# Seven-product pairs, halved plain pairs and residual rows kept in memory in the gate/up blocks of a hybrid decoder layer

## The chip, the cores and the metric

The kernel runs on one core of one Trainium2 chip. The metric is the device time of one execution in microseconds (us). The engines are TensorE (PE, and PEld for its weight loads), VectorE (DVE), ScalarE (ACT), GpSimd (POOL) and SyncE (SP, which here only issues transfers). Each engine runs its own instructions in a fixed order and waits on semaphores for the others.

## The reference

One decoder layer on 256 tokens of width 2048, in float32. The change touches the last two thirds of it:

```python
y = jnp.concatenate([y_lru, y_ret], axis=-1)
h = h + jnp.einsum('bse,ed->bsd', y, w_out[l])
u = rmsnorm(h, ln2_w[l])
ff = jax.nn.silu(jnp.einsum('bsd,df->bsf', u, w_ffn_gate[l])) * jnp.einsum('bsd,df->bsf', u, w_ffn_up[l])
h = h + jnp.einsum('bsf,fd->bsd', ff, w_ffn_down[l])
return rmsnorm(h, final_norm_w)
```

`w_out` is 2048 x 2048, gate and up are 2048 x 5632 each, `w_ffn_down` is 5632 x 2048. Ahead of it come a norm, one projection to 6144 columns, a gated linear recurrence and a chunked retention.

## The kernel before

**A product is three matmuls.** To keep float32 precision, every operand is split into a high part (a cast on ScalarE to a reduced format, `wh` for weights) and a low part (a subtraction on VectorE, `wl`), line 112 and line 113. A product of two tiles is then three matmuls, high x high, high x low and low x high (`three`, lines 670 to 672), each 128x128 of activations against 128x512 of weights.

**Blocks.** The output projection has blocks 0 and 1, gate/up has blocks 2 to 12 (11 blocks of 512 gate and 512 up columns), and the down projection has two more. A block goes through eight pairs of 256 weight rows. Such a pair is a 2x2 product: activations a11, a12, a21, a22 (two token tiles, two row tiles) against weights b11, b12 (gate), b21, b22 (up). A pair's weights come from memory as two loads of 128x1024 (512 KB each) into `raw` tiles, six buffers in a ring. The split makes `wh` and `wl` tiles of 128x1024; there are four buffers of each (pool `split`), and a buffer is free when the last matmul that reads it is done.

**Plain and seven-product pairs.** A plain pair ("p") is eight products, 24 matmuls. A pair in `SUMMED` is done with seven products, 21 matmuls, in two steps:
- "s" (class `Shared`, method `share`): four products, 12 matmuls, whose sums over all seven-product pairs of a block are needed in several outputs. They are done one block ahead of their own block. Both halves of the weights are loaded; b11 is split, VectorE then makes four sums of halves in place (`add`, line 648), and t1 with t3 (one 128x1024 tile), t2 (in the other half of b11's tile) and t4 (a tile of its own, `t4h`, `t4l`) are split.
- "d" (class `Direct`, method `direct`): three products, 9 matmuls, in the block itself. The second half of the weights is loaded and split once more (one 128x1024 tile); t4 is still there.

`STEPS` has one string for each block, which says in which order its own plain and direct steps and the next block's shared steps stand. The blocks 3 to 10 alternate `"pspsdpsdpsdp"` and `"psdpsdpsddp"`, with three and four seven-product pairs. A block ends with `post`: four operations on VectorE and two on ScalarE on the shared sums (lines 782 to 787), and the gate (lines 842 and 844).

**Order.** Steps are put into `program` in order, loads run three ahead of the step that needs them, and a scheduler then orders each engine's instructions. SyncE issues the weight loads in order; each waits until its raw buffer was read by its last subtraction.

**Residual rows.** `htok`, eight 128x512 float32 tiles (pool `resid`, 16 KB of each partition), hold the residual stream. They are last read in the first plain step of block 2 (transposed by `turn`) and not again before the down projection adds into them (line 888). At block 2 (`swap`) the pools of the recurrence are closed, and a pool `late` is opened for the norm weights `fw`, which SyncE loads.

Of the kernel before, what the change touches and what calls it, by code (L numbers as in the profile page):

```python
# [14 lines left out]
P = 128  # L15
# [13 lines left out]

SUMMED = ((), (4, 5), (2, 3)) + ((1, 2, 3), (0, 1, 2, 3)) * 4 + ((1, 2, 3), (1, 2, 3))
SUMMED_OUT, SUMMED_FFN = (4, 5), (0, 1, 2, 3)

PLAIN = ((4, 5, 6, 7, 0, 1, 2, 3),) * 2 + (tuple(range(8)),) * 11
STEPS = ("pppspppspp", "ppspdpsdpp", "pdpsdpspspp") + ("pspsdpsdpsdp", "psdpsdpsddp") * 4 + ("psdpsdpsdpp", "psdpsdpsdpp")


EARLY_DOWN = (0, 1, 2)
# [5 lines left out]
def tile_hymba_layer(ctx: ExitStack, tc: tile.TileContext, A: dict, out: bass.AP):  # L45
# [2 lines left out]

    cpool = ctx.enter_context(tc.tile_pool(name="consts", bufs=1))
    apool = ctx.enter_context(tc.tile_pool(name="acts", bufs=60))  # L50
    xpool = ctx.enter_context(tc.tile_pool(name="resid", bufs=8))
    rpool = ctx.enter_context(tc.tile_pool(name="raw", bufs=6))
    wpool = ctx.enter_context(tc.tile_pool(name="split", bufs=4))
    early = ctx.enter_context(ExitStack())
    epool = early.enter_context(tc.tile_pool(name="conv", bufs=2))
    tpool = early.enter_context(tc.tile_pool(name="tmp", bufs=6))
    late = []
    pmm = ctx.enter_context(tc.tile_pool(name="pmm", bufs=4, space=PSUM))
    paux = ctx.enter_context(tc.tile_pool(name="paux", bufs=4, space=PSUM))

# [7 lines left out]
        return apool.tile([P, 512], dt, tag="act", name=nm(name))  # L68

    def res_tile(name, dt=F32):  # L70
        return xpool.tile([P, 512], dt, tag="xh", name=nm(name))

    def late_tile(name, dt=F32):
        return late[0].tile([P, 512], dt, tag="late", name=nm(name))
# [40 lines left out]
    class Unit:  # L115
# [6 lines left out]
            self.h, self.l = [], []  # L122

        def load(self, j):
            raw = rpool.tile([P, 1024], F32, tag="raw", name=nm("raw"))
            h = wpool.tile([P, 1024], F32R, tag="wh", name=nm("wh"))
            l = wpool.tile([P, 1024], F32R, tag="wl", name=nm("wl"))
            n = 1024 // self.pieces
            for p in range(self.pieces):
                o = p * n  # L130
                nc.sync.dma_start(out=raw[:, o : o + n], in_=self.src[:, j * 1024 + o : j * 1024 + o + n])
                if self.before:
                    self.before(j * self.pieces + p)
            for p in range(self.pieces):
                o = p * n
                split(h[:, o : o + n], l[:, o : o + n], raw[:, o : o + n])
                if self.after:
                    self.after(j * self.pieces + p)
            self.h.append(h)
            self.l.append(l)  # L140
# [424 lines left out]
    v2 = cpool.tile([P, 2], F32, name="v2")  # L565
    turns = []

    def out_post(d):
# [12 lines left out]

        def post(c, ps):
            cb, t = 2 * d + int(c[2]) - 1, int(c[1]) - 1
            h = htok[cb, t]
            v.tensor_tensor(out=h, in0=ps, in1=h, op=ALU.add)
            act.activation(out=act_tile("junk"), in_=h, func=AF.Square, accum_out=sq2[:, t, cb : cb + 1])
            if t:
                turns.extend(lambda p=p: turn(p) for p in (2 * cb, 2 * cb + 1))
            if (cb, t) == (3, 1):
                v.tensor_reduce(out=v2, in_=sq2, axis=mybir.AxisListType.X, op=ALU.add)  # L590
                rsqrt_small(r2_tok, v2, 1.0 / D, 2)

        return post
# [10 lines left out]
    class Quad:  # L604
# [19 lines left out]
                self.parts[name] = h[:, n * 512 : n * 512 + 512], l[:, n * 512 : n * 512 + 512]  # L624

        def load(self, half):
            r = rpool.tile([P, 1024], F32, tag="raw", name=nm("raw"))
# [12 lines left out]
            self.add(r)  # L640
            self.cut(("t1", "t3"), self.ra)
            self.cut(("t2", "t4"), r)
# [80 lines left out]
    class Shared(Quad):  # L723
# [2 lines left out]
        hl = None, None  # L726

        def load(self, half):
            r = rpool.tile([P, 1024], F32, tag="raw", name=nm("raw"))
# [17 lines left out]
    class Direct(Quad):  # L747
# [6 lines left out]
            self.shared = shared  # L754

        def load(self, half):
            r = rpool.tile([P, 1024], F32, tag="raw", name=nm("raw"))
            nc.sync.dma_start(out=r, in_=self.src[:, 1024:2048])
            self.cut(("b22", "b21"), r)
            self.parts["t4"] = self.shared.parts["t4"]  # L760

    class Block:

# [26 lines left out]
            for c, a, b in DIRECT:  # L790
                three(self.ps[c], self.lefts[self.summed[m]][a], quad.parts[b], False, False, True)

        def plain(self, i, quad, first, last):
            ps, onto, seen = self.ps, bool(self.summed), set()
            for n, (c, a, b) in enumerate(LAST if last else EIGHT):
                if first and n == 4:
                    while turns:
                        turns.pop(0)()
# [275 lines left out]
    ]  # L1074
    down = Block(NB + 2, lambda i: A["w_down"][i], dl, None, "", EARLY_DOWN, make_left)
    for b, after in zip(blocks, blocks[1:] + [down]):
        if b.index == 2:
            program.append(([], swap))
        b.put(after)
        if b.index == NB:  # L1080
            program.append(([], load_fw))

    for d in range(2):
        down_block(d, down)
# [117 lines left out]
```

## Time and profile before

| | |
|---|---|
| three runs | 1085.74, 1085.87 and 1086.69 us, median 1085.87 |
| span of the profiled execution | 1084.4 us from its first to its last instruction |
| busy TensorE, VectorE, ScalarE | 99%, 88%, 61% of the span |
| granted TensorE clock | 1.00 in every window of 20 us |
| read from memory | 235.26 MB, 219 GB/s over the span |

The profiled execution's own time is its span and what lies around it; against the runs' median that is 1085.87 - 1084.4 = 1.5 us. In the views a line number is that of the kernel; a group is named out<-in by the program's tile names; "idle before" is the engine's own waiting, with what ended it. The timelines give start, length, engine, line, operation and count, and join equal neighbours. TensorE's matmuls overlap, so their lengths add up to more than their time: their price is the distance of their starts. The same holds, by less, for VectorE and ScalarE.

### The profile page before, as it was taken

Reading aid. Unit: us, or ns where it says so; the run is one execution under the profiler, and the core shown is the slowest. Engines: PE = TensorE matmul, PEld = TensorE weight load, DVE = VectorE, ACT = ScalarE, POOL = GpSimd, SP = SyncE. Lnnn points to the kernel's source line nnn. Section 1 sums busy time; section 2 is a strip of 40 time slices with the busy share of each in tenths; the row PEclk is TensorE's granted clock in tenths of the full one; section 3 lists DMA queues with packets and bytes.
Section 4 is the critical chain, followed back from the end, with each engine's and each line's share of the span. In section 5 each row is a group of like instructions: output and inputs, shape, how many; then the busy total and the mean of one; then the engine's idle time right before and its main releaser. Section 6 shows DMA issues by size and latency. Waiting matters only on the chain.

```text
span 1084.4 us, 14584 instructions
## 1 busy us (share of the span) xinstructions
PE 1074.2 (99%) x5101; PEld 899.5 (83%) x5101; DVE 953.5 (88%) x1371; ACT 660.9 (61%) x935; POOL 51.0 (5%) x61
## 2 busy tenths in 40 slices
PE   9999999999999999999999999999999999999997
PEld 7888888888888788888888888888888888888885
DVE  7789799988878889888998998999899899898986
ACT  7666644468746676565566566556556666655563
POOL 0612230000000000000000000000000000000001
PEclk9999999999999999999999999999999999999999
DMA  9964474444565567577677677686675756465652
GB/s 330 333 211 168 160 252 173 174 175 171 181 230 205 184 228 275 198 248 266 220 245 261 220 264 235 233 289 214 233 271 194 265 181 213 171 214 199 212 209 85
DMA packets 69274, 238.32 MB, mean 220 GB/s; under 512 B 7888, under 2 KB 8272, under 8 KB 69200
## 3 DMA queue, kind: packets, MB, share of 16 engines
q1 hardware_dynamic: 68400, 235.29, 62.7%
q0 software_dynamic: 512, 1.57, 0.4%
q8 instruction: 40, 0.66, 0.2%
q10 hardware_dynamic: 288, 0.52, 0.1%
q14 instruction: 34, 0.28, 0.1%
HBM read 235.26 MB, written 2.10 MB: 219 GB/s over the span
## 4 chain that ended last, share of the span: by engine, by line
PE 97%; DVE 1%; issue 1%; DMA 0%; ACT 0%; POOL 0%; SPq 0%; POOLq 0%; ACTq 0%
PE c L670 22%; PE c L672 22%; PE c L671 22%; PE fm L184 11%; PE fm L186 5%; PE tm L164 3%; PE tm L165 3%; PE tm L166 3%; PE p L672 1%; PE p L671 1%; PE p L670 1%; PE ft L833 1%; DMA raw<-in_w_v 0%; PE ht L576 0%; PE sc L482 0%
## 5 line engine op out<-in xcount | busy, mean ns | idle before, releaser
L112 ACT CAST wh<-raw 128x1024 fp32r<-128x1024 f32 (+1 forms) x490 | 460.9, 965 | 362.6 <-PE c L672 132.5
L113 DVE TENSOR_TENSOR wl<-raw,wh 128x1024 fp32r<-128x1024 f32 (+1 forms) x490 | 538.2, 1122 | 91.2 <-ACT wh L112 88.4
L671 PE MATMUL c<-wl,ah 128*128 128x512 f32 x850 | 331.0, 390 | 0.0
L672 PE MATMUL c<-wh,al 128*128 128x512 f32 x850 | 330.4, 389 | 0.0
L670 PE MATMUL c<-wh,ah 128*128 128x512 f32 x850 | 275.0, 391 | 0.2 <-ACT wh L112 0.2
L670 PEld LDWEIGHTS c<-wh,ah 128*128 128x128 f32 x850 | 159.4, 188 | 33.4 <-ACT wh L112 1.1
L672 PEld LDWEIGHTS c<-wh,al 128*128 128x128 f32 x850 | 159.6, 188 | 33.0
L671 PEld LDWEIGHTS c<-wl,ah 128*128 128x128 f32 x850 | 159.6, 188 | 32.7
L184 PE MATMUL fm<-u,wh 128*128 128x512 f32 x512 | 161.3, 396 | 0.0
L186 PEld LDWEIGHTS fm<-u,wl 128*128 128x128 f32 x512 | 96.0, 188 | 22.5
L186 PE MATMUL fm<-u,wl 128*128 128x256 f32 x512 | 101.1, 278 | 0.0
L184 PEld LDWEIGHTS fm<-u,wh 128*128 128x128 f32 x512 | 78.4, 189 | 0.3
L648 DVE TENSOR_TENSOR raw<-raw,raw 128x512 f32<-128x512 f32 x106 | 73.1, 690 | 2.8
L648 DVE TENSOR_TENSOR raw<-raw 128x512 f32<-128x512 f32 x106 | 72.7, 689 | 2.4
L671 PE MATMUL c<-wl,sh 128*128 128x512 f32 x176 | 68.5, 389 | 0.0
L672 PE MATMUL c<-wh,sl 128*128 128x512 f32 x176 | 68.0, 389 | 0.0
L670 PE MATMUL c<-wh,sh 128*128 128x512 f32 x176 | 60.4, 394 | 0.3 <-ACT sh L112 0.3
L165 PE MATMUL tm<-wl,u 128*128 128x512 f32 x128 | 48.8, 394 | 0.0
L166 PE MATMUL tm<-wh,u 128*128 128x512 f32 x128 | 48.7, 390 | 0.0
L164 PE MATMUL tm<-wh,u 128*128 128x512 f32 x128 | 47.3, 398 | 0.8 <-ACT u L288 0.8
L954 POOL TENSOR_TENSOR htok<-htok,fw 128x512 f32<-128x512 f32 x2 | 2.5, 1273 | 895.9 <-ACT junk L947 895.9
L670 PEld LDWEIGHTS c<-wh,sh 128*128 128x128 f32 x176 | 33.1, 188 | 7.3 <-ACT sh L112 0.7
(245 smaller groups left out, 1034.9 us busy)
## 6 DMA issues: line engine op xcount, KB each, us to landing
raw<-in_w_gu SPq DMA_DIRECT2D x212, 512.0 KB, 5.5
raw<-in_w_down SPq DMA_DIRECT2D x91, 512.0 KB, 4.3
raw<-in_w_out SPq DMA_DIRECT2D x34, 512.0 KB, 3.7
raw<-in_w_lx SPq DMA_DIRECT2D x16, 512.0 KB, 6.3
raw<-in_w_k SPq DMA_DIRECT2D x16, 512.0 KB, 3.5
raw<-in_w_q SPq DMA_DIRECT2D x16, 512.0 KB, 4.0
raw<-in_w_rg SPq DMA_DIRECT2D x16, 512.0 KB, 3.4
raw<-in_w_lg SPq DMA_DIRECT2D x16, 512.0 KB, 3.4
```

What stands on the lines that cost most here:

```text
L112: act.copy(out=dst_h, in_=src)
L113: v.tensor_tensor(out=dst_l, in0=src, in1=dst_h.bitcast(F32), op=ALU.subtract)
L164: pe.matmul(ps, ah, wh, start=first, stop=False)
L165: pe.matmul(ps, ah, wl, start=False, stop=False)
L166: pe.matmul(ps, al, wh, start=False, stop=last)
L184: pe.matmul(ps, wh, hl, start=n + i == 0, stop=False)
L186: pe.matmul(ps[:, :S], wl, hl[:, :S], start=False, stop=n + i == len(order) - 1)
L648: v.tensor_tensor(out=dst, in0=a, in1=b, op=ALU.add)
L670: pe.matmul(p, ah, bh, start=first, stop=False, skip_group_check=onto)
L671: pe.matmul(p, ah, bl, start=False, stop=False, skip_group_check=onto)
L672: pe.matmul(p, al, bh, start=False, stop=last, skip_group_check=onto)
L833: pe.transpose(pt[:, o : o + P], g[:, (2 * b + c) * P : (2 * b + c) * P + P], ident)
```

## The change

- `SUMMED`: block 3 has three seven-product pairs, blocks 4 to 11 have four each, block 12 three. Before, blocks 3 to 12 had three and four in turn, and three in 11 and 12.
- `STEPS`: seven blocks, 4 to 10, have the order `"psdhsdhsdhsdhp"`. The new step "h" (class `HalfOf`) is half a plain pair: one load, one split tile, four products, 12 matmuls. Two "h" make one pair.
- Raw tiles: from block 3 to block 11 a second pool `raw2` with six more buffers is used in turn with the first (`raw_tile`).
- Residual rows: in `out_post` each finished tile is also written to memory, `kept_rows`, from ScalarE's queue. The pool `resid` is closed with the others, now at block 3, and makes the room for `raw2`. After block 12 (`swap_back`) `raw2` is closed, and GpSimd's queue loads the eight tiles back and the norm weights after them.
- The split buffers stay four and four; the loads stay three ahead.

The diff, cut:

```diff
-SUMMED = ((), (4, 5), (2, 3)) + ((1, 2, 3), (0, 1, 2, 3)) * 4 + ((1, 2, 3), (1, 2, 3))
+SUMMED = ((), (4, 5), (2, 3), (1, 2, 3)) + ((0, 1, 2, 3),) * 8 + ((1, 2, 3),)
...
-STEPS = ("pppspppspp", "ppspdpsdpp", "pdpsdpspspp") + ("pspsdpsdpsdp", "psdpsdpsddp") * 4 + ("psdpsdpsdpp", "psdpsdpsdpp")
+STEPS = ("pppspppspp", "ppspdpsdpp", "pdpsdpspspp", "pspsdpsdpsdp") + ("psdhsdhsdhsdhp",) * 7 + ("psdpsdpsddp", "psdpsdpsdpp")
...
-    xpool = ctx.enter_context(tc.tile_pool(name="resid", bufs=8))
...
+    xpool = early.enter_context(tc.tile_pool(name="resid", bufs=8))
...
+    def raw_tile():
+        turn_of[0] += 1
+        pool_ = more[0] if more and turn_of[0] % 2 else rpool
+        return pool_.tile([P, 1024], F32, tag="raw", name=nm("raw"))
...
             act.activation(out=act_tile("junk"), in_=h, func=AF.Square, accum_out=sq2[:, t, cb : cb + 1])
+            act.dma_start(out=kept[cb, t], in_=h)
...
+    class HalfOf:
+        n_loads = 1
+
+        def __init__(self, quad, half):
+            self.quad, self.half = quad, half
+
+        def load(self, j):
+            self.quad.load(self.half)
...
-        def plain(self, i, quad, first, last):
+        def plain(self, i, quad, first, last, some=slice(None)):
...
-            for n, (c, a, b) in enumerate(LAST if last else EIGHT):
+            for n, (c, a, b) in enumerate((LAST if last else EIGHT)[some]):
...
+                elif kind == "h":
+                    at = self.steps[:k].count("h") % 2
+                    if not at:
+                        i = plain.pop(0)
+                        whole = Quad(self.src(i), False)
+                    quad = HalfOf(whole, at)
+                    some = slice(4 * at, 4 * at + 4)
+                    run = lambda i=i, quad=whole, some=some: self.plain(i, quad, False, False, some)
...
-            nc.sync.dma_start(out=fw[c], in_=A["final_norm_w"][c * 512 : c * 512 + 512].partition_broadcast(P))
+            pool.dma_start(out=fw[c], in_=A["final_norm_w"][c * 512 : c * 512 + 512].partition_broadcast(P))
...
         early.close()
+        more.append(extra.enter_context(tc.tile_pool(name="raw2", bufs=6)))
...
+    def swap_back():
+        extra.close()
         late.append(ctx.enter_context(tc.tile_pool(name="late", bufs=4)))
+        resid[0] = ctx.enter_context(tc.tile_pool(name="resid2", bufs=8))
+        for key in [(cb, t) for cb in range(4) for t in range(2)]:
+            htok[key] = res_tile("htok")
+            pool.dma_start(out=htok[key], in_=kept[key])
+        load_fw()
```

How the instructions move is shown at two places. The first is VectorE in the middle of a gate/up block of the kernel before: line 113 is a subtraction of a split (`wl_1131` holds t1 and t3, `wl_1136` a direct tile, `wl_1139`, `wl_1142` and `wl_1148` plain tiles), line 648 an add of a shared pair.

```order
L113 TENSOR_TENSOR wl_1128_5452<-raw_1126_5449,wh_1127_5451 128x512
L648 TENSOR_TENSOR raw_1126_5449<-raw_1126_5449 128x512
L648 TENSOR_TENSOR raw_1126_5449<-raw_1126_5449,raw_1129_5464 128x512
L648 TENSOR_TENSOR raw_1129_5464<-raw_1126_5449,raw_1129_5464 128x512
L648 TENSOR_TENSOR raw_1129_5464<-raw_1129_5464 128x512
L113 TENSOR_TENSOR wl_1131_5473<-raw_1126_5449,wh_1130_5472 128x1024
L113 TENSOR_TENSOR wl_1136_5483<-raw_1134_5480,wh_1135_5482 128x1024
L113 TENSOR_TENSOR wl_1128_5452<-raw_1129_5464,wh_1127_5451 128x512
L113 TENSOR_TENSOR t4l_1133_5477<-raw_1129_5464,t4h_1132_5476 128x512
L113 TENSOR_TENSOR wl_1139_5513<-raw_1137_5510,wh_1138_5512 128x1024
L113 TENSOR_TENSOR wl_1142_5519<-raw_1140_5516,wh_1141_5518 128x1024
L113 TENSOR_TENSOR wl_1148_5546<-raw_1146_5543,wh_1147_5545 128x1024
```

VectorE in the same place of the changed kernel, from the second "s" of a block to the third (line 119 is the subtraction now, line 657 the add; `wl_1510` holds t1 and t3, `wl_1515` is the direct tile, `wl_1518` the half plain one):

```order
L119 TENSOR_TENSOR wl_1503_7183<-raw_1501_7180,wh_1502_7182 128x512
L657 TENSOR_TENSOR raw_1501_7180<-raw_1501_7180 128x512
L657 TENSOR_TENSOR raw_1501_7180<-raw_1501_7180,raw_1508_7202 128x512
L657 TENSOR_TENSOR raw_1508_7202<-raw_1501_7180,raw_1508_7202 128x512
L657 TENSOR_TENSOR raw_1508_7202<-raw_1508_7202 128x512
L119 TENSOR_TENSOR wl_1510_7211<-raw_1501_7180,wh_1509_7210 128x1024
L119 TENSOR_TENSOR wl_1515_7230<-raw_1513_7227,wh_1514_7229 128x1024
L119 TENSOR_TENSOR wl_1518_7248<-raw_1516_7245,wh_1517_7247 128x1024
L119 TENSOR_TENSOR wl_1503_7183<-raw_1508_7202,wh_1502_7182 128x512
L119 TENSOR_TENSOR t4l_1512_7215<-raw_1508_7202,t4h_1511_7214 128x512
L119 TENSOR_TENSOR wl_1521_7254<-raw_1519_7251,wh_1520_7253 128x512
```

Between two shared pairs stood two plain tiles, and now stands one: the last row is already the next pair's b11.

The second place is TensorE at the same pair. Before, after the rows of the shared pair (`wh_1130`) and the direct tile (`wh_1135`), come those of a whole plain pair, whose first tile is `wh_1138`:

```order
L670 MATMUL c22_1092_5282<-wh_1130_5472,sh_758_3724 128x512 [waits Activation_49]
L670 MATMUL c21_1093_5286<-wh_1130_5472,sh_758_3724 128x512
L670 MATMUL c11_1018_4939<-wh_1135_5482,ah_755_3715 128x512 [waits Activation_49]
L670 MATMUL c12_1021_4951<-wh_1135_5482,sh_758_3724 128x512
L670 MATMUL c12_1094_5290<-wh_1127_5451,sh_758_3724 128x512 [waits Activation_49]
L671 MATMUL c22_1092_5282<-wl_1131_5473,sh_758_3724 128x512 [waits DVE_49]
L672 MATMUL c22_1092_5282<-wh_1130_5472,sl_759_3725 128x512
```

TensorE in the changed kernel, at the second "s" of a block, where the first row reads b11's cast, `wh_1509` is t1 and t3, `wh_1514` the direct tile and `wh_1517` the half plain one:

```order
L679 MATMUL c11_1504_7186<-wh_1502_7182,ah_741_3677 128x512 [waits Activation_49]
L680 MATMUL c11_1504_7186<-wl_1503_7183,ah_741_3677 128x512 [waits DVE_49]
L681 MATMUL c11_1504_7186<-wh_1502_7182,al_742_3678 128x512
L679 MATMUL c22_1505_7190<-wh_1509_7210,sh_744_3686 128x512 [waits Activation_49]
L679 MATMUL c21_1506_7194<-wh_1509_7210,sh_744_3686 128x512
L679 MATMUL c11_1423_6813<-wh_1514_7229,ah_741_3677 128x512 [waits Activation_49]
L679 MATMUL c12_1426_6825<-wh_1514_7229,sh_744_3686 128x512
L680 MATMUL c22_1505_7190<-wl_1510_7211,sh_744_3686 128x512 [waits DVE_49]
L681 MATMUL c22_1505_7190<-wh_1509_7210,sl_745_3687 128x512
L680 MATMUL c21_1506_7194<-wl_1510_7211,sh_744_3686 128x512
L681 MATMUL c21_1506_7194<-wh_1509_7210,sl_745_3687 128x512
L679 MATMUL c22_1424_6817<-wh_1517_7247,ah_837_4105 128x512 [waits Activation_49]
```

From the last matmul that reads the direct tile of the first "sdh" (`wh_1492`, whose buffer the cast of `wh_1502` takes) to the first that reads the next direct tile (`wh_1514`) are 25 matmuls; from one "s" to the next are 33, where before they were 45.

More of the change, by code (lines that the diff above doesn't have):

```diff
@@ L54, in tile_hymba_layer @@
     early = ctx.enter_context(ExitStack())
+    xpool = early.enter_context(tc.tile_pool(name="resid", bufs=8))
     epool = early.enter_context(tc.tile_pool(name="conv", bufs=2))
     tpool = early.enter_context(tc.tile_pool(name="tmp", bufs=6))
-    late = []
+    late, resid, more, turn_of = [], [xpool], [], [0]
+    extra = ExitStack()
     pmm = ctx.enter_context(tc.tile_pool(name="pmm", bufs=4, space=PSUM))
@@ L70, in res_tile @@
     def res_tile(name, dt=F32):
-        return xpool.tile([P, 512], dt, tag="xh", name=nm(name))
+        return resid[0].tile([P, 512], dt, tag="xh", name=nm(name))
+    def raw_tile():
+        turn_of[0] += 1
+        pool_ = more[0] if more and turn_of[0] % 2 else rpool
+        return pool_.tile([P, 1024], F32, tag="raw", name=nm("raw"))
     def late_tile(name, dt=F32):
@@ L124, in load @@
         def load(self, j):
-            raw = rpool.tile([P, 1024], F32, tag="raw", name=nm("raw"))
+            raw = raw_tile()
             h = wpool.tile([P, 1024], F32R, tag="wh", name=nm("wh"))
@@ L566, in tile_hymba_layer @@
     turns = []
+    kept = nc.dram_tensor("kept_rows", (4, 2, P, 512), F32, kind="Internal").ap()
     def out_post(d):
@@ L626, in load @@
         def load(self, half):
-            r = rpool.tile([P, 1024], F32, tag="raw", name=nm("raw"))
+            r = raw_tile()
             nc.sync.dma_start(out=r, in_=self.src[:, half * 1024 : half * 1024 + 1024])
@@ L728, in load @@
         def load(self, half):
-            r = rpool.tile([P, 1024], F32, tag="raw", name=nm("raw"))
+            r = raw_tile()
             nc.sync.dma_start(out=r, in_=self.src[:, half * 1024 : half * 1024 + 1024])
@@ L756, in load @@
         def load(self, half):
-            r = rpool.tile([P, 1024], F32, tag="raw", name=nm("raw"))
+            r = raw_tile()
             nc.sync.dma_start(out=r, in_=self.src[:, 1024:2048])
@@ L1067, in swap, with stop_more @@
         early.close()
-        late.append(ctx.enter_context(tc.tile_pool(name="late", bufs=4)))
+        more.append(extra.enter_context(tc.tile_pool(name="raw2", bufs=6)))
+    def stop_more():
+        more.clear()
+    def swap_back():
+        extra.close()
+        late.append(ctx.enter_context(tc.tile_pool(name="late", bufs=4)))
+        resid[0] = ctx.enter_context(tc.tile_pool(name="resid2", bufs=8))
[3 more added lines that the diff above has]
+        load_fw()
     blocks = [Block(d, lambda i, d=d: A["w_out"][8 * d + i], y, out_post(d), STEPS[d], SUMMED[d]) for d in range(2)]
@@ L1076, in tile_hymba_layer @@
     for b, after in zip(blocks, blocks[1:] + [down]):
-        if b.index == 2:
+        if b.index == 3:
             program.append(([], swap))
+        if b.index == NB + 1:
+            program.append(([], stop_more))
         b.put(after)
-        if b.index == NB:
-            program.append(([], load_fw))
+    program.append(([], swap_back))
     for d in range(2):
```

## The prediction

> **What bounds the kernel now.** The page comes first: the engines, then the chain.
>
> ```profile
> span 1084.4 us, 14584 instructions
> PE 1074.2 (99%) x5101; PEld 899.5 (83%) x5101; DVE 953.5 (88%) x1371; ACT 660.9 (61%) x935; POOL 51.0 (5%) x61
> ...
> PE 97%; DVE 1%; issue 1%; DMA 0%; ACT 0%; POOL 0%; SPq 0%; POOLq 0%; ACTq 0%
> ```
>
> TensorE is the chain, so a matmul less is its price less, unless TensorE has to wait. The price is read from TensorE's timeline: between these two starts lie 41 steps without a transpose.
>
> ```profile
> 557.23 0.39 PE L670 MATMUL c<-wh,ah 128*128 128x512 f32 x1
> ...
> 566.53 0.39 PE L672 MATMUL c<-wh,al 128*128 128x512 f32 x1
> ```
>
> 9.30 / 41 = 0.2268 us each (0.39 is the pipelined length). Then the steady part: the chain in order of time gives two starts of the same place two gate/up blocks apart, and the windows view shows what the engines did between.
>
> ```profile
> 523.38 1.15 PE c L670 x5
> ...
> 607.47 1.15 PE c L670 x5
> ```
>
> ```profile
> 523.38:607.47 84.09, 84.09 (x380) 69.70 (x380) 76.09 (x94) 49.87 (x66) 0.00 (x0) 1.00 0.72 244
> ```
>
> Columns: length, busy time of PE, PEld, DVE, ACT and POOL, granted clock (1.00), DMA share and GB/s. Two blocks are 363 product matmuls, 82.33 us; the other 1.76 us are 16 transposes, 0.88 a block. TensorE never waits. VectorE has 8.0 us in hand. The waits view of the same window says what VectorE and ScalarE wait for, and the last row, of the whole trace, how often on gate/up weights:
>
> ```profile
> ACT wh L112 <- DVE raw L648: 18.9, 7, 3.0
> ACT wh L112 <- PE c L672: 15.0, 13, 2.2
> DVE wl L113 <- ACT wh L112: 7.1, 6, 1.8
> ```
>
> ```profile
> ACT wh L112 <- DMA raw<-in_w_gu: 1.9, 3, 1.2
> ```
>
> The casts wait for VectorE's adds and for TensorE to release one of the four split buffers; VectorE waits behind the casts. Weights from memory cost 1.9 us in all, so six more raw buffers have at most that to win, and none of it is a wait of TensorE.
>
> **The change part by part.** *Matmuls.* Blocks 3 to 11 have 31 seven-product pairs, then 35. Each saves one product of three matmuls: 4 x 3 x 0.2268 = 2.72 us off TensorE.
>
> *VectorE's load.* Its price is best read as one stretch of the timeline without idle time:
>
> ```profile
> 545.60 1.83 DVE L113 TENSOR_TENSOR wl<-raw,wh 128x1024 fp32r<-128x1024 f32 x2 [0.66 <-ACT wh L112]
> 547.46 0.69 DVE L648 TENSOR_TENSOR raw<-raw 128x512 f32<-128x512 f32 x1
> 548.19 1.42 DVE L648 TENSOR_TENSOR raw<-raw,raw 128x512 f32<-128x512 f32 x2
> 549.64 0.69 DVE L648 TENSOR_TENSOR raw<-raw 128x512 f32<-128x512 f32 x1
> 550.25 2.95 DVE L113 TENSOR_TENSOR wl<-raw,wh 128x1024 fp32r<-128x1024 f32 x3
> 553.12 0.68 DVE L113 TENSOR_TENSOR t4l<-raw,t4h 128x512 fp32r<-128x512 f32 x1
> 553.72 1.22 DVE L113 TENSOR_TENSOR wl<-raw,wh 128x1024 fp32r<-128x1024 f32 x1
> ```
>
> From 545.60 to 553.72 stand three 1024-wide subtractions, three 512-wide ones and four adds: exactly what one "s", one "d" and one "h" ask for (s: two of 512 and t4, one of 1024, the adds; d and h: one of 1024 each). So "sdh" costs VectorE 8.12 us. From the starts, a 512-wide subtraction is 553.72 - 553.12 = 0.60, and a 1024-wide one (553.12 - 550.25 - 0.60) / 2 = 1.135. TensorE needs 12 + 9 + 12 = 33 matmuls, 7.48 us. The old "sdp" gave 45 matmuls, 10.21 us, for 8.12 + 1.135 = 9.26 us. The sign turns: inside the new stretch VectorE is the slower by 0.64 us each time.
>
> Over a whole block the books still balance. Six more operations work on the sums and the gate; their starts lie 0.60 and 0.66 apart:
>
> ```profile
> 561.61 0.69 DVE L787 TENSOR_TENSOR c<-c,p 128x512 f32<-128x512 f32 x1
> 562.21 0.74 DVE L844 SCALAR_TENSOR_TENSOR gated<-c,r_tok,gated 128x512 f32<-128x512 f32 x1
> 562.87 0.68 DVE L648 TENSOR_TENSOR raw<-raw 128x512 f32<-128x512 f32 x1
> ```
>
> VectorE: 4 x 8.12, two plain pairs 4 x 1.135, four operations of 0.60 and two of 0.66, together 40.7 us. TensorE: 180 x 0.2268 + 0.88 = 41.7. So the question is how far ahead VectorE may be when the stretch begins.
>
> *The lead.* Only four split buffers exist, and the change adds none; the raw ones stand before the casts. At the second "s" of a block, the cast of b11 must take the buffer of the direct tile before it. From the last matmul that reads that tile to the first that reads the new direct tile are 25 matmuls, 5.67 us. The chain beside them is priced from these rows (and VectorE's above):
>
> ```profile
> 544.09 0.39 PE L672 MATMUL c<-wh,sl 128*128 128x512 f32 x1
> ...
> 545.45 0.39 PE L672 MATMUL c<-wh,sl 128*128 128x512 f32 x1
> ...
> 552.93 0.39 PE L670 MATMUL c<-wh,ah 128*128 128x512 f32 x1
> ```
>
> ```profile
> 544.51 1.05 ACT L112 CAST wh<-raw 128x1024 fp32r<-128x1024 f32 x1 [1.53 <-PE c L672]
> 545.87 0.62 ACT L112 CAST wh<-raw 128x512 fp32r<-128x512 f32 x1 [0.30 <-PE c L672]
> 548.99 2.52 ACT L112 CAST wh<-raw 128x1024 fp32r<-128x1024 f32 x3 [2.49 <-DVE raw L648]
> 551.41 0.62 ACT L112 CAST t4h<-raw 128x512 fp32r<-128x512 f32 x1
> ```
>
> Matmul to cast 0.42 (544.09 to 544.51); b11's cast 0.62; cast to subtraction 0.04 (544.51 + 1.05 to 545.60); subtraction to first add 0.72 (547.46 less 545.60 + 1.135); first to second add 0.73; second add to the cast of t1, t3 0.80 (548.19 to 548.99); that to the direct tile's cast 0.95 (two such and one of 0.52 make 548.99 to 551.41); its length 1.05; and the start of TensorE behind a wait, from the one stall that shows it:
>
> ```profile
> 947.34 3.90 ACT L112 CAST wh<-raw 128x1024 fp32r<-128x1024 f32 x4 [1.63 <-DVE raw L648]
> ```
>
> ```profile
> 948.44 0.50 PE L670 MATMUL p<-wh,sh 128*128 128x512 f32 x1
> 948.78 0.39 PE L670 MATMUL c<-wh,ah 128*128 128x512 f32 x1
> ```
>
> The first cast ends at 948.39; TensorE starts at 948.44 and takes 0.34 to the next instead of 0.23: 0.16 lost. Sum 5.49. So at the second "s" TensorE is 0.18 us short of waiting. Checked on the kernel before: from 545.45, whose end released b11's cast of 545.87, to the direct tile's 552.93 lie 7.48 us, and that tile's cast, the second of the three, ends at 548.99 + 0.95 + 1.05 = 550.99: 1.9 us in hand, as the plain pair there makes room.
>
> In the third "s" TensorE waits 0.64 - 0.18 = 0.46 us, in the fourth 0.64 more: 1.10 us a block. Then come plain pairs, where TensorE is the slower, and VectorE runs up to the four buffers again and waits, so nothing is carried into the next block. Seven blocks (4 to 10) have this order: 7.7 us. The chain's sum is good to about 0.3 us either way, so a block costs 0.8 to 1.4 us, in all 5.6 to 9.8.
>
> [...] By the rows' full lengths "sdh" would be 3 x 1.22 + 3 x 0.68 + 4 x 0.69 = 8.46 us, the waits about 1.9 us a block, and the time 1096. The trace disagrees: the add of 549.64 takes 0.69, and the next operation starts at 550.25, 0.61 later.
>
> *Residual rows and weights.* Eight writes are issued from ScalarE's queue in the post of the two output blocks, each with casts queued behind it. An issue is not in the trace as busy time; against the 0.62 of a small cast eight of them are 5 us of ScalarE, at most four in a row, 2.5 us. The cast that stands last there was done long before its use:
>
> ```profile
> 388.37 1.06 ACT L112 CAST wh<-raw 128x1024 fp32r<-128x1024 f32 x1
> ```
>
> ```profile
> 397.44 0.39 PE L670 MATMUL c<-wh,ah 128*128 128x512 f32 x1
> ```
>
> It ends at 389.43 and is first read at 397.44: 8 us cover it, cost 0. The new buffers open once those rows are written, and SyncE then issues six loads ahead of a shared pair's second half. At 389 GB/s, the most that a window shows, six loads of 512 KB take 8.1 us:
>
> ```profile
> 20.00:40.00 20.00, 20.00 (x104) 17.02 (x103) 13.85 (x21) 14.99 (x23) 9.30 (x6) 1.00 1.03 389
> ```
>
> That half's buffer is free when the subtraction below ends (399.85), and the add of 407.23 wants it:
>
> ```profile
> 398.62 1.23 DVE L113 TENSOR_TENSOR wl<-raw,wh 128x1024 fp32r<-128x1024 f32 x1
> ...
> 407.23 1.42 DVE L648 TENSOR_TENSOR raw<-raw,raw 128x512 f32<-128x512 f32 x2
> ```
>
> That is 7.4 us against 8.1 and its own 1.35, so 0 to 2 us are lost here once; I take 0, for the rows are written before 399.85 and the burst is partly through by then. The norm weights' four loads leave SyncE's queue, where nothing of TensorE waited for them: 0. Reading rows and norm weights back is 3 MB on GpSimd's queue in block 12; the first reader of rows starts here, over 100 us later, cost 0:
>
> ```profile
> 953.57 0.69 DVE L888 TENSOR_TENSOR htok<-htok,part 128x512 f32<-128x512 f32 x1
> ```
>
> **Sum.** 1084.4 - 2.72 + 7.7 = 1089.4 span; what lies around the span (median 1085.87 less 1084.4, 1.5 us) stays: 1090.9, 5.0 slower.
>
> **Rivals.** (1) *The lead lasts*: the books balance over a block, TensorE has 2 x 0.64 = 1.28 us or more in hand at the second "s" where I count 0.18, and it never waits. For it speaks 40.7 against 41.7; against it the 15.0 us of casts that wait for TensorE's buffers, which shows that the lead is already at its limit. 1083.2, faster. It decides from a chain 1.1 us shorter than mine. (2) *Half a lead*: the chain is 0.4 to 1.0 us shorter, waits under 0.7 us a block, 1083.7 to 1088.0, the same. (3) *More waits*: the first "s" waits too, or the burst of loads holds VectorE, or VectorE is slower than the rows say: 1093 to 1100. That the change doesn't cut matmuls is excluded: TensorE's order has twelve fewer.
>
> **How the numbers follow.** Forecast 0.62, its own range 1088.8 to 1093.0 (-2.72 + 5.6 to 9.8); rival 1 0.13, rival 2 0.17, rival 3 0.08. Some 0.2% (2.2 us) is what a measurement of this kernel can tell from no change. Faster 0.13, same 0.17, slower 0.70. The range 1083.7 to 1095.0 leaves out rival 1 and the end of rival 3.
>
> **What would show it.** Right: in blocks 4 to 10 a period of about 42.8 us (before 42.05), with TensorE waiting for ScalarE's casts of 1024 in the third and fourth "s", and VectorE without idle time between the second and the fourth; the wait of VectorE ahead of a block's second "s" stays, near 2 us. Wrong: a period near 41.7 and no wait of TensorE; or waits on memory.

## The result, and the profile after

The changed kernel takes 1092.34 us (median of four runs, 1092.10 to 1092.88), the kernel before, timed beside it, 1085.94 (1085.74 to 1086.69). The ratio is 1.0059, with a 95% interval of 1.0046 to 1.0072: 6.4 us slower, where 5.0 were forecast. The page of the changed kernel, with the same three lines that were shown of before:

```profile
span 1090.4 us, 14638 instructions
PE 1076.0 (99%) x5089; PEld 893.8 (82%) x5089; DVE 969.5 (89%) x1399; ACT 667.2 (61%) x947; POOL 58.0 (5%) x73
...
PE 86%; DMA 5%; DVE 5%; ACT 2%; issue 1%; POOL 0%; SPq 0%; ACTq 0%; POOLq 0%
```

Twelve matmuls are gone, and yet TensorE's share of the chain fell from 97% to 86%: the chain now runs through other engines. The busy shares hardly moved, and nothing could be read from them. The chain in order of time gives the same place of a block six blocks apart:

```profile
527.45 0.69 PE c L679 x3
...
784.70 0.69 PE c L679 x3
```

(784.70 - 527.45) / 6 = 42.88 us a block. TensorE's own work is 180 x 0.2268 + 0.88 = 41.70, so 1.17 us a block are waits and the slower steps right behind them. TensorE's timeline in one of these blocks shows them, at the third shared pair and at the fourth (the number in brackets is the idle time, with what ended it):

```profile
628.05 0.63 PE L679 MATMUL c<-wh,sh 128*128 128x512 f32 x2
628.86 0.50 PE L679 MATMUL c<-wh,ah 128*128 128x512 f32 x1 [0.18 <-ACT wh L118]
629.20 0.40 PE L679 MATMUL c<-wh,sh 128*128 128x512 f32 x1
```

```profile
636.04 0.73 PE L679 MATMUL c<-wh,sh 128*128 128x512 f32 x2
636.98 0.51 PE L679 MATMUL c<-wh,ah 128*128 128x512 f32 x1 [0.21 <-ACT wh L118]
637.32 0.39 PE L679 MATMUL c<-wh,sh 128*128 128x512 f32 x1
```

From 628.05 to 629.20 lie three steps, 0.68 us at full pace; they take 1.15, so 0.47 are lost. From 636.04 to 637.32 it is 1.28, so 0.60. The remaining 0.1 lies in single steps of the block. The idle time in brackets is smaller, because a matmul's modelled length covers part of the gap, and because the step behind a wait is slow too (628.86 to 629.20, 0.34 instead of 0.23): the loss is read from starts. The second row of each fence is the first that reads the direct tile, whose cast on ScalarE has only just ended. Behind that cast stands VectorE, in its timeline of the same block:

```profile
616.44 0.69 DVE L119 TENSOR_TENSOR wl<-raw,wh 128x512 fp32r<-128x512 f32 x1 [1.72 <-ACT wh L118]
```

```profile
628.07 4.09 DVE L119 TENSOR_TENSOR wl<-raw,wh 128x1024 fp32r<-128x1024 f32 x4
...
636.19 2.35 DVE L119 TENSOR_TENSOR wl<-raw,wh 128x1024 fp32r<-128x1024 f32 x2
```

VectorE waits 1.72 us ahead of the block's second shared pair. After that it has no idle time to the fourth, and from one pair's t1, t3 subtraction (628.07) to the next one's (636.19) it takes 8.12 us. TensorE's two waits end 628.86 and 636.98, 8.12 apart: there TensorE goes at VectorE's pace.

One wait more stands outside these blocks, at the end of block 11, where block 12 begins; below it is called block 12's wait. ScalarE's and TensorE's timelines there:

```profile
818.64 0.62 ACT L118 CAST sh<-s 128x512 fp32r<-128x512 f32 x1 [3.53 <-DVE s L560]
...
823.03 0.50 PE L679 MATMUL c<-wh,ah 128*128 128x512 f32 x1 [0.91 <-ACT wh L118]
```

ScalarE waits 3.53 us for VectorE to sum the activations of the down projection's first shared pair, and the cast that TensorE needs is queued behind. With the slow step behind it this costs 1.2 us. Together: -2.7 for the matmuls, 7 x 1.17 = 8.2, and 1.2 make 6.7; the spans differ by 6.0. Of the 0.7 between, 0.5 lie ahead of what was changed in the gate/up blocks: at the start of block 4 TensorE's profile stands at 483.00 where that of the kernel before stands at 483.48, after the same matmuls. The four runs of the kernel before differ by 0.95 among themselves.

**A trap in the chain.** It names DMA for 5% of the span, as if weights came late. Chain, then SyncE's issues:

```profile
631.59 4.28 DMA raw<-in_w_gu
635.89 1.05 ACT wh L118
```

```profile
613.00 0.33 SPq L767 DMA_DIRECT2D raw<-in_w_gu  x1
```

The cast of 635.89 is that of the direct tile. It starts when the cast ahead of it ends. Its own load is the one of line 767, issued at 613.00, 23 us earlier; the load of 631.59 belongs to a later pair. Tiles stand in the view without their numbers, so a landing that happens to precede a cast can be taken for its cause. That memory isn't the cause is shown by the run *steps*, below.

### The profile page after: what moved, and what is told of

Read it like the earlier page. It is cut to its first block, busy times and chain, and to the rows that moved or that the text cites. A ratio compares the mean times of both kernels' runs of the same rounds, so it can differ in the third digit from the quotient of the medians.

```text
span 1090.4 us, 14638 instructions
## 1 busy us (share of the span) xinstructions
PE 1076.0 (99%) x5089; PEld 893.8 (82%) x5089; DVE 969.5 (89%) x1399; ACT 667.2 (61%) x947; POOL 58.0 (5%) x73
## 4 chain that ended last, share of the span: by engine, by line
PE 86%; DMA 5%; DVE 5%; ACT 2%; issue 1%; POOL 0%; SPq 0%; ACTq 0%; POOLq 0%
PE c L679 19%; PE c L680 18%; PE c L681 18%; PE fm L190 11%; PE fm L192 5%; DMA raw<-in_w_gu 5%; DVE wl L119 3%; PE tm L170 3%; PE tm L171 3%; PE tm L172 3%; DVE raw L657 2%; ACT wh L118 2%; PE p L681 1%; PE p L680 1%; PE p L679 1%
## 5 line engine op out<-in xcount | busy, mean ns | idle before, releaser
L118 ACT CAST wh<-raw 128x1024 fp32r<-128x1024 f32 (+1 forms) x498 | 466.0, 959 | 354.1 <-DVE raw L657 131.0
L680 PE MATMUL c<-wl,ah 128*128 128x512 f32 x826 | 322.2, 390 | 0.0
L681 PE MATMUL c<-wh,al 128*128 128x512 f32 x826 | 321.6, 390 | 0.0
L681 PEld LDWEIGHTS c<-wh,al 128*128 128x128 f32 x826 | 155.1, 188 | 32.0
L657 DVE TENSOR_TENSOR raw<-raw,raw 128x512 f32<-128x512 f32 x114 | 78.7, 690 | 2.9
L657 DVE TENSOR_TENSOR raw<-raw 128x512 f32<-128x512 f32 x114 | 78.3, 690 | 2.7
L680 PE MATMUL c<-wl,sh 128*128 128x512 f32 x192 | 75.1, 391 | 0.0
L681 PE MATMUL c<-wh,sl 128*128 128x512 f32 x192 | 74.4, 390 | 0.0
L679 PE MATMUL c<-wh,sh 128*128 128x512 f32 x192 | 69.9, 399 | 0.3 <-ACT sh L118 0.3
L680 PEld LDWEIGHTS c<-wl,sh 128*128 128x128 f32 x192 | 36.1, 188 | 9.5 <-DVE wl L119 2.6
```

What stands on the lines that cost most here:

```text
L118: act.copy(out=dst_h, in_=src)
L657: v.tensor_tensor(out=dst, in0=a, in1=b, op=ALU.add)
L679: pe.matmul(p, ah, bh, start=first, stop=False, skip_group_check=onto)
L680: pe.matmul(p, ah, bl, start=False, stop=False, skip_group_check=onto)
L681: pe.matmul(p, al, bh, start=False, stop=last, skip_group_check=onto)
```

## The experiments

The theory: in a stretch "sdh" VectorE needs 8.12 us where TensorE needs 7.48, and four split buffers keep VectorE from starting the stretch far enough ahead. The rivals: the order of the instructions, and memory.

### Which part, and what cures it

**split6** has a fifth and a sixth split buffer, each in the room of two raw ones.

```diff
+    def split_tiles():
+        turn_of[1] += 1
+        pool_ = more[1] if more and turn_of[1] % 3 == 0 else wpool
+        return [pool_.tile([P, 1024], F32R, tag=g, name=nm(g)) for g in ("wh", "wl")]
...
-        more.append(extra.enter_context(tc.tile_pool(name="raw2", bufs=6)))
+        more.append(extra.enter_context(tc.tile_pool(name="raw2", bufs=2)))
+        more.append(extra.enter_context(tc.tile_pool(name="split2", bufs=2)))
```

> Six split buffers in blocks 3 to 11 where there were four (two raw ones fewer for each: raw2 has two instead of six), order of the steps unchanged. My theory (VectorE needs 8.12 us for a stretch that TensorE does in 7.48, and four split buffers keep it from being far enough ahead): the two waits of a block, 0.48 and 0.61 us, go, 7 x 1.09 = 7.6 us less than the changed kernel's 1092.3, so 1084.7, and 1083.5 if block 12's wait of 1.2 us goes too. Rival A (the order of the instructions makes TensorE wait for each shared pair's casts, however many buffers): 1092.3. Rival B (the loads are late, as the chain of waits names 4.7% of DMA): with eight raw buffers instead of twelve 1093 or more.

Measured 1083.79 (before 1086.29 beside it; ratio 0.9975, 0.9966 to 0.9985): the waits are gone, block 12's too, and the kernel is faster than both. But the scheduler, given other buffers, also wrote another order for every engine, so this run alone doesn't tell buffers from order.

**order** keeps the buffers.

```diff
-("psdhsdhsdhsdhp",) * 7
+("psdhsdpsdhsdp",) * 7
```

> The same steps in another order, psdhsdpsdhsdp: a whole plain pair after every second direct step, so that a stretch in which VectorE is slower by 0.64 us is followed by one in which it is faster by 0.95. Buffers, matmuls and VectorE's work unchanged. My theory: no stretch begins with less than the 0.18 us in hand that the second one has now, so no wait in blocks 4 to 10: 1092.3 - 7.6 = 1084.7. Rival A (each shared pair's casts hold TensorE by their place in the order): 1089 to 1092, the waits stay at each shared pair. Rival B (late loads): 1092.

Measured 1089.63 (ratio 1.0027, 1.0017 to 1.0036), 2.7 us under the changed kernel and 4.9 over what the theory gave. (In this run the second half of the halved pair is multiplied with the next pair's activations; the work is the same.) The waits at the third and fourth shared pair are gone, as the theory says, but a new one stands at the start of every block, ScalarE's and TensorE's rows:

```profile
562.96 0.59 ACT L805 COPY c<-q 128x512 f32<-128x512 f32 x1 [0.84 <-DVE q L804]
...
563.60 0.50 PE L679 MATMUL c<-wh,ah 128*128 128x512 f32 x1 [0.29 <-ACT c L805]
```

Only "dp" stands now between the last shared pair and the next block, not "dhp", and the post on the shared sums isn't through when the next block adds to them. From 562.92, where the matmul ahead starts, to 563.60 are 0.68 us instead of 0.23; with the slow step behind it 0.57 are lost a block, 4 us in seven, and block 12's wait is still there. Halving the pairs has a use that the prediction had not seen.

**memory** has the pairs and steps of before and the whole memory part of the change; **steps** is the reverse.

```diff
-SUMMED = ((), (4, 5), (2, 3), (1, 2, 3)) + ((0, 1, 2, 3),) * 8 + ((1, 2, 3),)
+SUMMED = ((), (4, 5), (2, 3)) + ((1, 2, 3), (0, 1, 2, 3)) * 4 + ((1, 2, 3), (1, 2, 3))
```

> Only the memory part of the change: residual rows written out and read back, six more raw buffers, norm weights on GpSimd's queue; pairs and steps as before. My theory: costs nothing, 1085.9 as the kernel before (1085.5 to 1086.5), no new wait of TensorE. Rival B (rows, their issues on ScalarE's queue, or the burst of loads cost time): 1087 to 1088, with the 1.2 us of block 12 in it.

> Only the pairs and steps of the change, with six raw buffers and the residual rows left on the chip. My theory: all of the loss is here, 1092.3 as the changed kernel, block 12's wait of 1.2 us with it; six raw buffers are enough. Rival B (the memory part is what costs): 1084 to 1087. If six raw buffers are too few for this order, as the change seems to hold: over 1094, with waits on loads.

Measured: *memory* 1086.98, ratio 1.0005 (0.9996 to 1.0014), no new wait of TensorE. *steps*: 1094.06, ratio 1.0064 (1.0051 to 1.0077), the changed kernel's within its interval. TensorE has the same order in it as in the changed kernel, VectorE too but for two rows, and the waits stand at the same places of each block, block 12's with them. Both medians lie a little off what was expected: *memory* is 0.7 us above the kernel before beside it (1086.29), between the two expectations, and *steps* is 1.4 us further above it than the changed kernel was, just over the 1094 of the last rival. The waits on loads that this rival needs are not there: from 484 to 828 us ScalarE waits for gate/up weights once, 0.8 us. So the loss is in pairs and steps, and the six raw buffers, for which the rows were moved, cost or save nothing that these runs can tell.

### Four runs that said something else than they were asked

**light** leaves out one of VectorE's adds, **split5** and **split5_rows** ask how many buffers are wanted, **heavy6** asks how far six carry.

```diff
-            for dst, a, b in ((b11, b11, b12), (b12, b12, b22), (b22, b11, b22), (b21, b22, b21)):
+            sums = ((b11, b11, b12), (b12, b12, b22), (b22, b11, b22), (b21, b22, b21))
+            for dst, a, b in sums[: 3 if more else 4]:
```

> The changed kernel with four split buffers, but without the last of the four adds of each shared pair in gate/up (t4 is then not the sum that it should be, the rest is unchanged). VectorE's stretch falls from 8.12 by 0.73 to 7.39 us, TensorE's stays 7.48. My theory (pace and lead): both waits of a block go, 7.6 us less than 1092.3, so 1084.7, and 1083.5 if block 12's wait goes as well. Rival A (TensorE waits for the cast of t1 and t3, which stands behind the second add, so that the fourth add doesn't matter): 1092.

```diff
-        more.append(extra.enter_context(tc.tile_pool(name="raw2", bufs=6)))
+        more.append(extra.enter_context(tc.tile_pool(name="raw2", bufs=4)))
+        more.append(extra.enter_context(tc.tile_pool(name="split2", bufs=1)))
```

> Five split buffers instead of four (raw2 has four instead of six). My theory: one more buffer lets VectorE be one more tile ahead, some 9 to 12 matmuls or 2.0 to 2.7 us of TensorE; the three stretches of a block need 0.18 - 3 x 0.64 = 1.7 us more than there was, so one buffer is enough: 1083.5 to 1084.5, as with six (1083.8). Rival (only two more are enough): the fourth shared pair still waits, 1085 to 1088.

> Pairs, steps and the fifth split buffer, with nothing of the memory part: six raw buffers, residual rows left on the chip, the norm weights loaded after block 12 so that their room can hold the fifth buffer. My theory: raw buffers limit nothing here, so the same as with five split buffers and ten raw ones: 1083.5 to 1084.5. Rival B (more lead needs more loads in flight, and six raw buffers don't hold them): 1086 or more, with casts waiting for loads.

```diff
+            if more:
+                v.tensor_tensor(out=act_tile("idle"), in0=b22, in1=b21, op=ALU.add)
```

> Six split buffers, and one more 512-wide add per shared pair of gate/up that nobody reads. By VectorE's books a block then has 40.7 + 4 x 0.73 = 43.6 us against TensorE's 41.7. My theory: buffers carry a lead only as long as the block's books balance, so the period becomes 43.6, 1.9 a block, in seven blocks 13 us more than 1083.8: 1097 (1094 to 1100). Rival C (with six buffers VectorE's work is hidden whatever it is): 1084.

Measured: 1107.47 (ratio 1.0193, 1.0178 to 1.0207), 1106.66 (1.0184, 1.0170 to 1.0197), 1104.97 (1.0169, 1.0155 to 1.0183) and 1110.50 (1.0221, 1.0207 to 1.0235). All four missed, and none by a few us. Less work on VectorE made the kernel 15 us slower. The reason is in ScalarE's timeline of *light*:

```profile
494.82 0.62 ACT L118 CAST t4h<-raw 128x512 fp32r<-128x512 f32 x1 [4.71 <-DMA raw<-in_w_gu]
495.34 3.46 ACT L118 CAST wh<-raw 128x1024 fp32r<-128x1024 f32 x4
```

Without its add, t4's cast is ready as soon as its load lands, and the scheduler put it ahead of the cast of t1 and t3, which TensorE needs. There it waits 4.71 us for the load, and everything behind it waits too; the run has 8 such waits, 33.2 us in all. In *split5*, ScalarE and TensorE at a block's end:

```profile
525.67 0.59 ACT L810 COPY c<-q 128x512 f32<-128x512 f32 x1
...
526.31 0.80 PE L684 MATMUL c<-wh,ah 128*128 128x512 f32 x1 [2.17 <-ACT c L810]
```

The post on the sums is queued behind casts, and one of them (521.58) had waited 0.99 us for TensorE to release a split buffer. So these edits changed the order as well as what they meant to change, and the order cost more. *heavy6* in particular says nothing on how far six buffers carry: VectorE waits for ScalarE there again (16.8 us between 500 and 800), so VectorE's work alone doesn't set its time.

### The same with the order held

From here each instruction of VectorE, ScalarE and TensorE is tied behind its predecessor in the changed kernel (`ORDER` is that order, as a table), so that an edit changes nothing else.

```diff
+    info = mybir.DependencyInfo(mybir.DependencyClass.NoSync, mybir.DependencyReason.DATA)
+    for name, moves in json.loads(zlib.decompress(base64.b85decode(ORDER))).items():
+        engine = getattr(mybir.EngineType, name)
+        own = [i for i in nc.cur_bb.bb.instructions if i.engine == engine]
+        rows = [own[k + m] for k, m in enumerate(moves)]
+        for a, b in zip(rows, rows[1:]):
+            tc.add_manual_dep(b, a.name, info, reason="order")
```

> Six split buffers and eight raw ones as in the run of that name, but VectorE, ScalarE and TensorE are made to run the changed kernel's instructions in exactly the changed kernel's order (each instruction is tied behind its predecessor there). Only the buffers differ from the changed kernel. My theory (pace and lead): the waits of blocks 4 to 10 go and block 12's too, 1083.5 (1083 to 1085). Rival D (the order that the scheduler wrote for six buffers was what helped, not the buffers): 1092, the waits stay.

Measured 1084.32 (before 1086.57; ratio 0.9980, 0.9971 to 0.9988). One block of its windows view (columns as before: length, busy PE, PEld, DVE, ACT, POOL, clock, DMA share, GB/s), and VectorE's timeline in it:

```profile
525.84:567.55 41.71, 41.71 (x190) 34.57 (x189) 39.34 (x51) 24.54 (x35) 0.00 (x0) 1.00 0.73 249
```

```profile
532.06 4.09 DVE L169 TENSOR_TENSOR wl<-raw,wh 128x1024 fp32r<-128x1024 f32 x4
...
540.18 4.09 DVE L169 TENSOR_TENSOR wl<-raw,wh 128x1024 fp32r<-128x1024 f32 x4
...
548.30 4.09 DVE L169 TENSOR_TENSOR wl<-raw,wh 128x1024 fp32r<-128x1024 f32 x4
```

VectorE still takes 8.12 us for each stretch (532.06, 540.18, 548.30), in the same order, and TensorE waits nowhere in the block: 41.71, which is its own work. Two buffers more are all that differs on these engines (and four raw buffers fewer). The lead is what was missing: rival D falls. Of block 12's wait 0.8 us stay, where *split6* with its own order has none, so that one is partly order.

> The changed kernel's order tied down in the same way, five split buffers, six raw ones, residual rows on the chip. My theory: one buffer gives 2.0 to 2.7 us more lead where 1.7 are wanted, and the 1105 of the run without the tie came from the other order: 1083.5 to 1084.7. Rival (five buffers are too few, as that run seemed to say): 1088 to 1105. Rival B (six raw buffers too few once VectorE runs further ahead): 1086 or more, casts waiting for loads.

Measured 1095.91 (ratio 1.0087, 1.0073 to 1.0101): 9 us better than without the tie, so the order did cost that much, but worse than with four: the wait shown below comes every 43.24 us (552.50, then 595.74), where a block of the changed kernel takes 42.88. ScalarE's and TensorE's timelines at the fourth shared pair:

```profile
544.93 0.63 ACT L164 CAST wh<-raw 128x512 fp32r<-128x512 f32 x1
551.40 3.47 ACT L164 CAST wh<-raw 128x1024 fp32r<-128x1024 f32 x4 [5.85 <-PE c L724]
```

```profile
550.93 0.39 PE L724 MATMUL c<-wh,sl 128*128 128x512 f32 x1
...
552.50 0.73 PE L722 MATMUL c<-wh,sh 128*128 128x512 f32 x2 [0.73 <-ACT wh L164]
```

The cast of t1 and t3 (551.40) takes the buffer of the previous pair's b11 and t2, and t2's last matmul, the one of 550.93, is nearly the last of that pair. With four buffers the same cast takes the previous direct tile's, which was free 2.7 us before it was wanted. So "one buffer more is one tile more lead" was wrong: what counts is which tile hands its buffer on. That six raw buffers serve a longer lead stays open, since there was none.

> The changed kernel with its four split buffers and its own order tied down, without the fourth add of each shared pair in gate/up (t4 is then not the sum it should be), so that no other instruction moves. My theory: VectorE's stretch is 7.39 us against TensorE's 7.48, so both waits of a block go, 7.6 us off 1092.3: 1084.7 (1084 to 1086). Rival A (it is the place of the cast of t1 and t3 behind the second add, whatever VectorE's sum): 1092.

Measured 1091.38 (ratio 1.0040, 1.0026 to 1.0054): one us, not 7.6 (1.6 if each is taken against the kernel before beside it: 4.8 over it, where the changed kernel is 6.4 over). Here the theory seemed to fall. VectorE's and ScalarE's timelines:

```profile
585.86 4.10 DVE L164 TENSOR_TENSOR wl<-raw,wh 128x1024 fp32r<-128x1024 f32 x4 [0.47 <-ACT wh L163]
...
591.92 1.42 DVE L703 TENSOR_TENSOR raw<-raw,raw 128x512 f32<-128x512 f32 x2
593.81 2.36 DVE L164 TENSOR_TENSOR wl<-raw,wh 128x1024 fp32r<-128x1024 f32 x2 [0.47 <-ACT wh L163]
```

```profile
588.14 0.63 ACT L163 CAST t4h<-raw 128x512 fp32r<-128x512 f32 x1
588.66 0.63 ACT L163 CAST wh<-raw 128x512 fp32r<-128x512 f32 x1
592.72 3.47 ACT L163 CAST wh<-raw 128x1024 fp32r<-128x1024 f32 x4 [3.43 <-DVE raw L703]
```

The stretch is 7.95 us, not 7.39, and VectorE waits 0.47 ahead of t1 and t3, for a cast that waits for VectorE's own second add. The fourth add had stood in that gap. Either the gap explains it, or a round through the four buffers takes 7.95 whatever VectorE does. ScalarE's rows speak for the gap: between the two stretches it waits for VectorE's add, and its cast of b11 (588.66) follows t4's without waiting for a buffer. So do TensorE's waits, which fell to 0.29 and 0.44 us in six of the seven blocks: a stretch of 7.95 is 0.47 slower than TensorE's 7.48, and with a lead of 0.18 that gives 0.29 at the third shared pair and 0.47 at the fourth. Leaving out the first add, which stands ahead of the cast, tells these apart:

```diff
-            for dst, a, b in sums[: 3 if more else 4]:
+            for dst, a, b in sums[1 if more else 0 :]:
```

> As the run without the fourth add, with the changed kernel's order and its four split buffers, but without the first add of each shared pair in gate/up instead (t1 then lacks a part). The fourth add stood in a gap that VectorE has anyway: after the second add ScalarE casts t1 and t3, and VectorE's next subtraction starts 1.20 us after the second add ended; without the fourth add 0.47 us of that is idle, so VectorE's stretch was 7.95 instead of 7.39. The first add stands ahead of that cast and fills no gap. My theory (VectorE's pace): the stretch is 8.12 - 0.73 = 7.39, under TensorE's 7.48, and both waits of a block go: 1084.7 (1084.0 to 1085.5), block 12's wait stays. Rival A2 (the round through four split buffers takes 7.95 whatever VectorE has to do): 1091, as without the fourth add.

Measured 1085.20 (before 1086.52; ratio 0.9988, 0.9979 to 0.9997), 7.1 us under the changed kernel. VectorE:

```profile
575.07 4.10 DVE L164 TENSOR_TENSOR wl<-raw,wh 128x1024 fp32r<-128x1024 f32 x4
...
582.34 4.29 DVE L164 TENSOR_TENSOR wl<-raw,wh 128x1024 fp32r<-128x1024 f32 x4
...
589.81 4.30 DVE L164 TENSOR_TENSOR wl<-raw,wh 128x1024 fp32r<-128x1024 f32 x4
```

7.47 us a stretch, which is TensorE's pace. The stretch ahead, in which VectorE is not yet held up, takes 7.27 (575.07 to 582.34), less than the 7.39 expected; from then on the same four tiles take 4.29 instead of 4.10, so now VectorE is the one that is held up. TensorE waits nowhere in blocks 4 to 10; only block 12's wait is left. With four buffers and the same order, it was VectorE's pace.

## Why the prediction was right

- **Fewer matmuls, 2.72 us.** It fits: *pin_split6*, where the waits are gone but for 0.8 us, is 2.25 faster than before, and *split6*, without any, 2.50.
- **The stretch, 8.12 against 7.48.** Right to the hundredth: 628.07 to 636.19, and again in *pin_split6*. The estimate of 8.46 by the rows' full lengths falls, as the prediction held: the trace after has the same overlap, the add of 627.46 takes 0.69, and the next operation starts at 628.07, 0.61 later.
- **The lead, 0.18 us at the second shared pair.** Right in its effect: no wait there, 0.47 at the third (forecast 0.46), 0.60 at the fourth (0.64), 1.17 a block (1.10). That the four buffers are what limits it was only argued in the prediction; *pin_split6* shows it. The 0.18 itself was not measured.
- **VectorE's wait ahead of the second shared pair**, near 2 us: 1.72.
- **Residual rows, weights and norm weights at 0**: *memory* lies between 0.4 us less and 1.5 us more than before, by its interval, which is no difference that can be told. The burst of six loads (issued from 393.49 to 395.82) cost TensorE no wait: the waits view from 380 to 440 us has none.
- **What was missing** is the 1.2 us at the end of block 11. The prediction looked at blocks 4 to 10 and priced the blocks around them by their matmuls alone. There VectorE also has the down projection's sums to make, with a direct step more in the same block (block 11 has four seven-product pairs now and had three). This term, and 0.5 us more in the seven blocks, less the 0.7 above, of which only 0.2 stay unexplained, is the difference in the spans between the forecast's 5.0 and the 6.0 measured. That these terms partly cancel is luck. A further 0.4 is what lies around the span: 1092.34 - 1090.4 = 1.9, where 1.5 were taken. That 1.5 was a profiled span set against the median of other runs; where one run has both, it is 1.72 to 1.81 for the kernel before (25 runs beside *split6*) and 1.8 to 1.9 for the changed one.
- **Rival 1, the lead lasts**: it needed the buffers that *split6* has; its 1083.2 is close to that run's 1083.8. **Rival 2, half a lead**, needs waits under 0.7 us a block: they are 1.17. **Rival 3**, more waits: TensorE waits neither at the second shared pair nor on loads, and VectorE's 8.12 is what the rows said.

Open is how much VectorE could be given with six buffers, and whether a fifth buffer, handed on in a better order, is enough.

## What to carry to other kernels

Two engines whose work balances over a block can still stall in a stretch where the feeding engine is the slower (here 8.12 us against 7.48, and 1.17 us lost a block), unless the buffers between them hold the stretch's whole deficit (with two more, 41.71 us a block and no wait of TensorE); so sum each stretch between two points where the lead is known, and look at which tile frees the buffer that the next cast takes. Where a scheduler orders the instructions, an edit that removes work or adds a buffer also writes a new order, and here that was worth up to 16 us (*light* 1107.5 against *pin_light* 1091.4): hold the order before reading a cause from such a run.

## What the runs showed of the hardware

**In *split5* TensorE fell to about half pace behind a wait of 2.17 us; in *light* it did not behind one of 2.00.** *split5*, windows and timeline behind the wait (the clock is the column behind POOL's):

```profile
526.00:530.00 4.00, 3.69 (x10) 2.96 (x11) 4.00 (x7) 0.26 (x1) 0.00 (x0) 0.57 0.68 248
```

```profile
526.90 0.63 PE L685 MATMUL c<-wl,ah 128*128 128x512 f32 x1
527.33 0.63 PE L686 MATMUL c<-wh,al 128*128 128x512 f32 x1
527.76 0.63 PE L684 MATMUL c<-wh,ah 128*128 128x512 f32 x1
...
529.74 0.39 PE L686 MATMUL c<-wh,al 128*128 128x512 f32 x1
```

The granted clock is 0.57, and the matmuls from 526.90 to 529.46 are 0.43 apart, not 0.23. From the wait's end (526.31) to 529.74 lie eight steps, 1.81 us at full pace; they take 3.43, so 1.6 us come on top of the wait. The waits view of the run has five waits on this post, 9.2 us in all and 2.2 the longest, and three more stretches of it show a low clock:

```profile
614.60:618.00 3.40, 3.40 (x9) 2.71 (x10) 3.40 (x7) 0.00 (x0) 0.00 (x0) 0.54 0.68 249
703.00:706.00 3.00, 3.00 (x9) 2.32 (x10) 3.00 (x6) 0.00 (x0) 0.00 (x0) 0.61 0.78 285
791.40:795.00 3.60, 3.60 (x11) 2.87 (x12) 3.60 (x7) 0.00 (x0) 0.00 (x0) 0.64 0.73 236
```

By length and clock that is an estimate of 1.6, 1.2 and 1.3 us (3.40 x 0.46, 3.00 x 0.39, 3.60 x 0.36). In *light*, behind its longest wait on weights, the 2.00 us that end at 496.44, the clock stays at 1.00:

```profile
496.50:499.50 3.00, 2.78 (x11) 1.83 (x12) 3.00 (x4) 2.63 (x4) 0.00 (x0) 1.00 0.14 49
```

In the changed kernel, whose longest wait on gate/up weights is the 0.91 at 823.03, it is 1.00 too (from 823 to 827). In *heavy6*, from 500 to 800 us, where no wait of TensorE is longer than 1.9, it is 0.98 on average. So the length of a wait alone does not decide, and what else does was not shown. Over the whole profiled execution the granted clock is 0.991 in *split5* and *heavy6*, 0.994 in *split5_rows*, 0.997 in *light*, and 0.998 or 0.999 in the changed kernel and the other experiments.

**In *pin_light* a sum on VectorE that ScalarE had to cast before VectorE went on cost 1.20 us of latency**, from the end of the second add to the start of the subtraction. The second add starts at 591.92 and takes 0.69, the cast starts at 592.72, and the subtraction at 593.81; one cast of this size takes 1.05 (that of 635.89 in the changed kernel). Work that filled this gap was nearly free: taking out an add of 0.73 us there shortened the stretch by only 0.17, from 8.12 to 7.95.
